# Late query tiles, context and mixing moved one head on; layer 1's output projection by token groups, its last norms woven with values

## The chip, the cores and the metric

The kernel runs on one core of a Trainium2 chip. The metric is the time of one execution in device microseconds; the median of three runs stands for the kernel. TensorE (PE in the profile) multiplies, VectorE (DVE), ScalarE (ACT) and GpSimd (POOL) work on elements, SyncE (SP) issues most DMAs.

## The reference

One inference step of a two-layer network over 1024 sample tokens and 128 prompt tokens, width 1024, all float32:

```python
for i in range(DEPTH):                       # DEPTH = 2
    sh1, sc1, g1, sh2, sc2, g2 = ada_modulation(cond, ada_w[i], ada_b[i])     # one set for prompt, one for sample
    h = modulate(x, norm_mix[i], sh1, sc1)
    if i % 2 == 0:     # pooling mixer of 4 channel groups beside latent attention of 8 heads, one output projection
        m = concatenate([pool_mixer(a_in, ...), attn]) @ w_out
    else:              # neighbourhood attention of 16 heads with learned bias, plus all prompt keys
        q, k, v = na_qkv(h, w_in_l1, na_q_norm, na_k_norm)                    # q and k normed for each head
        m = attn @ w_out_l1
    x = x + g1 * m
    x = x + g2 * channel_mixer(modulate(x, norm_mlp[i], sh2, sc2), mlp1[i], mlp2[i])   # squared relu, 4096 wide
```

`channel_mixer(h, w1, w2)` is `square(relu(h @ w1)) @ w2`. Queries and keys get an RMS norm over each head; prompt tokens attend to prompt tokens alone, sample tokens to sample and prompt.

## The kernel before

Activations lie with channels on the 128 partitions and the 1152 tokens along the free dimension, as eight tiles (KD = 8). Tokens are cut into three chunks of 384 (CH, NCH = 3) or four of 288 (HC); two chunks of 288 make a token group of 576. A float32 product is made from a high and a low part of each operand by three matmuls (`mm3`: low by high, high by low, high by high), so operands are split: ScalarE or VectorE casts the high part, VectorE or GpSimd subtracts it. `wsplit` does that for a weight chunk: a DMA of 512 KB to `wr`, a cast to `wh` (L160), a subtraction to `wl` (L161). Rings hold 3 `wr` and 4 each of `wh` and `wl`. Other buffers come from 36 slots of SBUF, `S.alloc` and `S.free`.

The program is written as generators; `weave` takes steps of several of them in proportion to the numbers beside them, and a scheduler orders each engine's queue from that by its own estimates. The order on each engine is thereafter fixed, and engines wait for each other by semaphores. PSUM tiles come from three pools, `pa`, `pb`, `pc`.

Layer 0. `query_tile(t)` norms one of six query tiles: for each chunk a pair of matmuls over 8 rows spreads the heads' factors over the partitions (`ps_b`, L707 and L708), VectorE multiplies (L808, L810), then the tile is split and stored (`split_store`, two DMAs). Tiles 0 to 3 hold the plain part of the heads' queries, two heads each, 4 and 5 the rotated part. All six run before the attention. Then `value_gen` (`ps_v`, L840 to L844) is woven with `max_units(0)`: for each 128 queries and each chunk one matmul (`ps_m`, L1073) and one reduction on VectorE (L1074), 24 units a head. `put_max` then transposes the maxima (`ps_mt`, L1059) and sends them over two DMAs on POOL's queue, `mrow<-row` and `qh<-mrow`, to row 96 of `qh`. `attend_units` makes scores from three matmuls (`ps_st`, L1108, L1111, and L1112, which reads that row), exponentials on ScalarE, and values (`ps_pv`, L1115). Each head h is woven with the maxima of head h + 2 (head 0 with those of 1 and 2), head 0 with `ctx0` (the prompt's attention) and head 1 with `mix` (pooling's matmuls). From head 1 on `background()` also runs `ada_gen`: VectorE makes the rest of layer 0's modulation from streamed weights (L200).

Layer 1. Queries and keys are made in four groups of four tiles; after each its norm block runs: sums of squares (`ps8`), `head_rstd` on VectorE (L252 to L704, to `r8h`, `r8l`), pairs of 8-row matmuls and products (L1266), three chunks by four tiles; then splits and stores. After group 3's, `value_gen1` (36 units of 24 matmuls of 256 columns, L1427 to L1429) is woven with `na_max` of heads 0 and 1. Of the 16 heads' output pairs, 0 to 6 go over HBM (`od`).

Output projection of layer 1. `split_acts` splits a pair in whole (`oh`, `ol`, L937 and L938). `out_first` takes pairs 0 to 3 over all tokens, 24 tiles of 12 matmuls of 384; 8 (OA) of them are woven with head 15. `out_second` takes pairs 4 to 7, 32 tiles of 12 matmuls of 288, chunk by chunk; from chunk 2 on it steps `operand_gen`, which makes the seven operands of the MLP's first products from the first group's tokens, each split at L352 and L353. Layer 0's projection has another form already: `split_groups` splits a pair by token group (`oa`, L914 and L915), and `out_group(0, g)` takes all eight pairs at once, 24 matmuls of 288 a tile; it runs group 0, then group 1 beside `operand_gen`. The MLP (`ps`, L446 to L482) starts with products of those operands.

Of the kernel before, what the change touches and what calls it, by code (L numbers as in the profile page):

```python
# [13 lines left out]
ALU = mybir.AluOpType  # L14
# [18 lines left out]
XS, PSH, OW, OA, OB = (11, 11, 12, 12, 13, 13, 14, 14), (14, 14, 15, 15), 10, 8, 6  # L33
# [57 lines left out]
def hybrid_kernel(ctx: ExitStack, tc: tile.TileContext, I, O):  # L91
# [783 lines left out]

    def out_first(layer, acts):
        for q in range(4):
            ws = wout_chunk(layer, 0, q)
            for mi in range(2):
                for ch in range(NCH):  # L880
                    ps = PS("ps_o")[:, :CH]
                    mm3(ps, ws[mi], acts, ch * CH, ch * CH + CH)
                    residual(x, 2 * q + mi, ch, ps, layer, 0)
                    yield

    def out_second(layer, acts):
        ws = [wout_chunk(layer, 1, q) for q in range(4)]
        st, right, ops, og = {}, [], {}, None
        for ch in range(4):
            for m in range(KD):  # L890
                if ch == 3 or ch == 2 and m in (3, 6):
                    next(og, None)
                ps = PS("ps_o", ("pa", "pc")[m % 2])[:, :HC]
                mm3(ps, ws[m // 2][m % 2], acts, ch * HC, ch * HC + HC)
                for a, b, i in chunk_parts(ch, HC):
                    nc.vector.scalar_tensor_tensor(x[m][:, a:b], ps[:, a - ch * HC:b - ch * HC], adav(layer, 2, m, i),
                                                   x[m][:, a:b], op0=ALU.mult, op1=ALU.add)
            if ch < 2:
                st[ch] = norm_stats(x, ch, HC)
            if ch == 1:  # L900
                og = operand_gen(ops, quad_apply(x, 0, layer, st[0]), right)
            elif ch == 2:
                right.extend(quad_apply(x, 1, layer, st[1]))
# [27 lines left out]

    def split_acts(ops):
        acts = []
        for o in ops:
            a = (S.alloc("oh", F32R), S.alloc("ol", F32R))
            acts.append(a)
            nc.vector.tensor_copy(a[0], o)  # L937
            nc.vector.tensor_sub(a[1], o, a[0])  # L938
            S.free(o)
        return acts  # L940

    def free_acts(acts):
        for a in acts:
            S.free(*a)
# [193 lines left out]
    for h in range(8):  # L1138
# [13 lines left out]
        if h in (0, 1):  # L1152
            gs.append(((ctx0, 8), (mix, 14))[h])
# [79 lines left out]
    r8 = S.alloc("r8h", F32R), S.alloc("r8l", F32R)  # L1233
    silu_load()
    for g in range(4):
# [16 lines left out]
        for ch in range(NCH):  # L1252
            cs = slice(ch * CH, ch * CH + CH)
            ps8 = PS("ps8", "pb")[0:8, :CH]
            for t in range(4):
                square_sum(ps8, t, raw[t][:, cs], t == 0, t == 3)
            head_rstd(ps8, 64, cs, nts[(NCH * g + ch) % 2], r8, rows)
        for ch in range(NCH):
            for t in range(4):
                wn = "naq" if t < 2 else "nak"  # L1260
                pp_ = pq if t < 2 else pk
                ps = PS("ps_b", "pb")[:, :CH]
                bcast(ps, t, r8, slice(ch * CH, ch * CH + CH), rows)
                for a, b, i in chunk_parts(ch):
                    o = pp_[:, pairs[t] * P:pairs[t] * P + P] if i else raw[t][:, a:b]
                    nc.vector.scalar_tensor_tensor(o, raw[t][:, a:b], V(wn), ps[:, a - ch * CH:b - ch * CH],  # L1266
                                                   op0=ALU.mult, op1=ALU.mult)
        for t in range(4):
            hi, lo = fhs[t % 2], raw[t].bitcast(F32R)
            nc.scalar.copy(hi[:, :NS], raw[t][:, :NS])  # L1270
            nc.vector.tensor_sub(lo[:, :NS], raw[t][:, :NS], hi[:, :NS])
            dst, o = (qd, 0) if t < 2 else (kd, P)
            dma(dst[0][pairs[t], :, o:o + NS], hi[:, :NS])
            dma(dst[1][pairs[t], :, o:o + NS], lo[:, :NS])
# [133 lines left out]


    vt = []  # L1410

    def value_gen1():
        for qt in range(4):
            ws = [wsplit(I["wv1"][qt, i]) for i in range(2)]
            fs = slice(qt * 256, qt * 256 + 256)
# [241 lines left out]
```

## Time and profile before

| | us |
|---|---|
| median of 3 runs | 2985.34 (2983.98 to 2985.49) |
| the profiled execution | 2996.6 |
| its span on the core | 2994.7 |
| TensorE busy | 2909.3 (97%) |
| VectorE busy | 2151.7 (72%) |
| ScalarE busy | 1321.2 (44%) |
| GpSimd busy | 329.3 (11%) |

The mean clock granted to TensorE was 0.977 of full speed. A busy share counts the time in which an instruction ran on the engine; matmuls overlap each other, so their own durations are longer than the distance between their starts, and pace is read from the starts or from counts in a window. Names in the rows are the program's, `out<-in`; `ps_b` is an output in PSUM, `bl`, `bh` the low and high part of an MLP operand.

### The profile page before, as it was taken

The page shows a single profiled execution, that of the slowest core. Times are in us where ns is not written, and L with a number is a line of the kernel's source. Part 1 is how long each engine was busy: PE and PEld are TensorE (multiplying, and loading weights), DVE is VectorE, ACT ScalarE, POOL GpSimd, SP SyncE. Part 2 cuts the span into 40 slices and gives each one's busy share as a digit, 9 for nine tenths or more (in the row PEclk, how much of TensorE's full clock was granted, in tenths as well). Part 3 has the DMA queues.
Part 4 walks back from the last instruction along what each step waited for, and adds up shares of the span by engine and source line. Part 5 has one row for each costly group of instructions (what it writes and reads, how often), then busy time and mean ns, then how long its engine had stood idle before and what let it go on. Part 6 is the DMA issues. An engine that isn't in the chain of part 4 may idle for free. (4 is left out here: it accounts for less than half of the span.)

```text
span 2994.7 us, 46426 instructions
## 1 busy us (share of the span) xinstructions
PE 2909.3 (97%) x18302; PEld 2610.2 (87%) x18302; DVE 2151.7 (72%) x3923; ACT 1321.2 (44%) x2136; POOL 329.3 (11%) x238
## 2 busy tenths in 40 slices
PE   7999999999999999999999999998989999999999
PEld 4955666799999999999988897666989999999999
DVE  5977863477778899786898524667587678877775
ACT  5463444345355544354644423444244445453433
POOL 2004010141000020000221000111020000200000
PEclk9997999999999999999999999898989999999999
DMA  6527521222232344233555325775213222332322
GB/s 236 170 86 254 144 76 41 77 77 88 84 105 77 101 141 148 78 99 92 170 204 183 116 101 128 194 187 165 70 36 99 80 91 85 117 101 78 98 78 89
DMA packets 117435, 347.59 MB, mean 116 GB/s; under 512 B 16697, under 2 KB 37801, under 8 KB 117218
## 3 DMA queue, kind: packets, MB, share of 16 engines
q1 hardware_dynamic: 114674, 340.76, 36.9%
q0 software_dynamic: 2544, 3.87, 0.4%
q8 instruction: 144, 2.36, 0.3%
q14 instruction: 73, 0.60, 0.1%
HBM read 296.54 MB, written 46.85 MB: 115 GB/s over the span
## 5 line engine op out<-in xcount | busy, mean ns | idle before, releaser
L477 PE MATMUL ps<-mh,wl 128*128 128x288 f32 x2048 | 599.8, 294 | 0.0
L478 PE MATMUL ps<-mh,wh 128*128 128x288 f32 x2048 | 595.6, 295 | 0.0
L476 PE MATMUL ps<-ml,wh 128*128 128x288 f32 x2048 | 590.4, 295 | 2.6 <-DVE x L482 1.4
L446 PE MATMUL ps<-bl,wh 128*128 128x288 f32 x1792 | 534.4, 299 | 16.1 <-DVE bl L353 5.2
L447 PE MATMUL ps<-bh,wl 128*128 128x288 f32 x1792 | 530.9, 296 | 0.0
L448 PE MATMUL ps<-bh,wh 128*128 128x288 f32 x1792 | 529.2, 295 | 0.0
L477 PEld LDWEIGHTS ps<-mh,wl 128*128 128x128 f32 x2048 | 384.2, 188 | 0.1
L476 PEld LDWEIGHTS ps<-ml,wh 128*128 128x128 f32 x2048 | 380.1, 188 | 3.6 <-DVE x L482 1.4
L478 PEld LDWEIGHTS ps<-mh,wh 128*128 128x128 f32 x2048 | 382.4, 188 | 0.0
L482 DVE SCALAR_TENSOR_TENSOR x<-ps,ada,x 128x288 f32<-128x288 f32 (+2 forms) x640 | 270.8, 451 | 122.7 <-PE ps L478 121.5
L446 PEld LDWEIGHTS ps<-bl,wh 128*128 128x128 f32 x1792 | 337.9, 189 | 20.5 <-issue 9.3
L448 PEld LDWEIGHTS ps<-bh,wh 128*128 128x128 f32 x1792 | 339.7, 190 | 0.0
L447 PEld LDWEIGHTS ps<-bh,wl 128*128 128x128 f32 x1792 | 338.8, 189 | 0.2
L160 ACT CAST wh<-wr 128x1024 fp32r<-128x1024 f32 x188 | 197.1, 1049 | 190.2 <-PE ps L448 77.3
L419 ACT CAST wh<-s 128x512 fp32r<-128x512 f32 x256 | 146.1, 618 | 278.6 <-PE ps L478 194.9
L161 DVE TENSOR_TENSOR wl<-wr,wh 128x1024 fp32r<-128x1024 f32 x144 | 179.2, 1248 | 60.1 <-ACT wh L160 60.1
L200 DVE CUSTOM_DVE_ANT_0 trash<-wada,silu 128x1024 bf16<-128x1024 f32 x160 | 206.1, 1288 | 13.3 <-DMA wada<-in_wada 6.9
L419 ACT CAST wh<-wr 128x1024 fp32r<-128x1024 f32 (+1 forms) x128 | 106.9, 835 | 199.7 <-PE ps L478 135.7
L161 POOL TENSOR_TENSOR wl<-wr,wh 128x1024 fp32r<-128x1024 f32 x44 | 117.2, 2670 | 689.8 <-ACT wh L160 689.8
L420 DVE TENSOR_TENSOR wl<-s,wh 128x512 fp32r<-128x512 f32 x232 | 157.2, 709 | 3.7 <-ACT wh L419 1.5
L1115 PE MATMUL ps_pv<-p,vt 128*128 128x512 f32 x288 | 147.7, 596 | 0.1
L1074 DVE TENSOR_REDUCE stat<-ps_m 128x1 f32<-128x384 f32 x192 | 98.6, 551 | 65.2 <-PE ps_m L1073 64.9
(321 smaller groups left out, 6044.2 us busy)
## 6 DMA issues: line engine op xcount, KB each, us to landing
wr<-in_w SPq DMA_DIRECT2D x256, 512.0 KB, 3.7
wada<-in_wada SPq DMA_DIRECT2D x48, 512.0 KB, 3.5
wada<-in_wada0t SPq DMA_DIRECT2D x32, 512.0 KB, 3.7
wr<-in_win SPq DMA_DIRECT2D x24, 512.0 KB, 4.5
wr<-in_wout SPq DMA_DIRECT2D x24, 512.0 KB, 4.3
kk<-kd SPq DMA_DIRECT2D x32, 288.0 KB, 7.3
wadan<-in_wada SPq DMA_DIRECT2D x16, 512.0 KB, 8.8
ta<-in_bias_q SPq DMA_DIRECT2D x16, 512.0 KB, 4.4
```

What stands on the lines that cost most here:

```text
L160: nc.scalar.copy(hi, r)
L161: (nc.gpsimd if e else nc.vector).tensor_sub(lo, r, hi)
L200: nc.vector.tensor_tensor_reduce(trash, r[:, :D], silu[i][:, :D], scale=1.0, scalar=0.0, op0=ALU.mult, op1=ALU.add, accum_out=a)
L419: nc.scalar.copy(h, src)
L420: (nc.gpsimd if j in EDGE and min(ps) in EDGE_POOL else nc.vector).tensor_sub(l, src, h)
L446: nc.tensor.matmul(ps, wh[:, a], hl[:, b], start=k == 0, stop=False)
L447: nc.tensor.matmul(ps, wl[:, a], hh[:, b], start=False, stop=False)
L448: nc.tensor.matmul(ps, wh[:, a], hh[:, b], start=False, stop=k == 3)
L476: nc.tensor.matmul(ps, wh, hl, start=kk == 0, stop=False)
L477: nc.tensor.matmul(ps, wl, hh, start=False, stop=False)
L478: nc.tensor.matmul(ps, wh, hh, start=False, stop=kk == 3)
L482: nc.vector.scalar_tensor_tensor(x[m][:, a:b], ps[:, a - ch * HC:b - ch * HC], g, x[m][:, a:b], op0=ALU.mult, op1=ALU.add)
```

## The change

Three places. In layer 0 only tile 1 still runs after 4 and 0; tiles 5, 2 and 3 become `late_queries`, woven with head 0. `ctx0` goes with head 1, `mix` with head 2, and the ada units start with head 2. In layer 1 the norm block becomes a generator, `norm_group`; that of group 3 is woven with the first nine units of `value_gen1`, and 27 units remain beside `na_max`. The output projection of layer 1 goes by token groups: `out_first` makes pairs 0 to 3 for group 0 alone (16 tiles of 12 matmuls of 288, 10 of them with head 15), `out_second` adds pairs 4 to 7 for group 0, then takes all eight pairs for group 1 (16 tiles of 24 matmuls) beside `operand_gen`, one step for two tiles. For that all eight weight chunks are loaded and split a second time.

```diff
-XS, PSH, OW, OA, OB = (11, 11, 12, 12, 13, 13, 14, 14), (14, 14, 15, 15), 10, 8, 6
+XS, PSH, OW, OA, OB = (11, 11, 12, 12, 13, 13, 14, 14), (14, 14, 15, 15), 10, 10, 6
...
-    for t in (1, 5, 2, 3):
-        run(query_tile(t, nc.gpsimd))
-    S.free(*rk8, bcs)
+    run(query_tile(1, nc.gpsimd))
+    def late_queries():
+        for t in (5, 2, 3):
+            yield from query_tile(t, nc.gpsimd)
+        S.free(*rk8, bcs)
+        yield
...
-        if h == 1:
+        if h == 2:
             silu_load()
             bg.append(chain(ada_gen(0, range(16 + 8 * NEARLY, 48)), free_silu()))
...
-        if h in (0, 1):
-            gs.append(((ctx0, 8), (mix, 14))[h])
+        if h < 3:
+            gs.append(((late_queries(), 13), (ctx0, 8), (mix, 14))[h])
...
+        norm = norm_group(g, raw, rows, pairs)
+        if g < 3:
+            run(norm)
+        else:
+            vg = value_gen1()
+            weave((norm, 10), (islice(vg, 9), 9))
...
-    weave((value_gen1(), 36), (chain(na_max(0, tls[0]), na_max(1, tls[1])), 10))
+    weave((vg, 27), (chain(na_max(0, tls[0]), na_max(1, tls[1])), 10))
...
     def out_first(layer, acts):
         for q in range(4):
             ws = wout_chunk(layer, 0, q)
             for mi in range(2):
-                for ch in range(NCH):
-                    ps = PS("ps_o")[:, :CH]
-                    mm3(ps, ws[mi], acts, ch * CH, ch * CH + CH)
-                    residual(x, 2 * q + mi, ch, ps, layer, 0)
+                for ch in range(2):
+                    out_tile(layer, 2 * q + mi, ch, ws[mi], acts, 0)
                     yield
...
     def out_second(layer, acts):
         ws = [wout_chunk(layer, 1, q) for q in range(4)]
-        for ch in range(4):
+        st = {}
+        for ch in range(2):
             for m in range(KD):
-                if ch == 3 or ch == 2 and m in (3, 6):
-                    next(og, None)
...
+                out_tile(layer, m, ch, ws[m // 2][m % 2], [a[0] for a in acts[4:]], 1)
+            st[ch] = norm_stats(x, ch, HC)
+        for a in acts[4:]:
+            S.free_ap(a[0][0])
+        ops = {}
+        og = operand_gen(ops, quad_apply(x, 0, layer, st[0]), quad_apply(x, 1, layer, st[1]))
+        n = 0
+        for q in range(4):
+            ws = [wout_chunk(layer, half, q) for half in range(2)]
+            for mi in range(2):
+                for ch in (2, 3):
+                    out_tile(layer, 2 * q + mi, ch, [w for half in range(2) for w in ws[half][mi]], [a[1] for a in acts], 1)
+                    n += 1
+                    if n % 2 == 0:
+                        next(og, None)
...
-            acts = split_acts(pairs)
-            of = out_first(1, acts)
+            acts = [split_groups(o) for o in pairs]
+            of = out_first(1, [a[0] for a in acts])
```

`out_tile` makes one tile of 288 tokens by `mm3` and adds it to `x` on VectorE. Line numbers in the changed program differ: L1073 becomes L1069, L1059 L1055, L1108 to L1115 L1104 to L1111, L1427 to L1429 L1283 to L1285, L896 L880.

The first place is TensorE's queue between the transposing matmul of head 0's maxima and the first score matmul that reads them (L1112). Before:

```order
L1073 MATMUL ps_m<-kh_2107,qh_2106 128x384
L1059 MATMUL ps_mt<-ident,stat 8x128
L1073 MATMUL ps_m<-kh_2114,qh_2113 128x384 x2
L1108 MATMUL ps_st<-qh_2106,kl_2193 128x512
L1111 MATMUL ps_st<-ql_2192,kh_2107 128x512
L1073 MATMUL ps_m<-kh_2114,qh_2113 128x384 x3
L1108 MATMUL ps_st<-qh_2106,kl_2193 128x512
L1111 MATMUL ps_st<-ql_2192,kh_2107 128x512
L1073 MATMUL ps_m<-kh_2114,qh_2113 128x384 x13
L1112 MATMUL ps_st<-qh_2106,kh_2107 128x512 x3
L1073 MATMUL ps_m<-kh_2114,qh_2113 128x384 x3
L1115 MATMUL ps_pv<-p_2364,vt_241_2093 128x512
```

In the changed kernel, where that matmul is L1108:

```order
L1055 MATMUL ps_mt<-ident,stat 8x128
L1069 MATMUL ps_m<-kh_2114,qh_2113 128x384 x2
L1104 MATMUL ps_st<-qh_2106,kl_2139 128x512
L1107 MATMUL ps_st<-ql_2138,kh_2107 128x512
L1069 MATMUL ps_m<-kh_2114,qh_2113 128x384 x2
L707 MATMUL ps_b<-rkh_1463,bcs_1407 128x384
L708 MATMUL ps_b<-rkl_1464,bcs_1407 128x384
L1069 MATMUL ps_m<-kh_2114,qh_2113 128x384
L1104 MATMUL ps_st<-qh_2106,kl_2139 128x512
L1107 MATMUL ps_st<-ql_2138,kh_2107 128x512
L1069 MATMUL ps_m<-kh_2114,qh_2113 128x384 x3
L1108 MATMUL ps_st<-qh_2106,kh_2107 128x512 x3
```

Eight maxima and a broadcast pair stand between them in place of 18 maxima, and the other late pairs are spread through head 0.

The second is TensorE's queue in the norm block of group 3 (L707, L708) and the first values (`ps_v`). Before, from the last sum of squares on:

```order
L327 MATMUL ps_16527<-sql,sel8r 8x384
...
L1429 MATMUL ps_v_16828<-wh,hh_948_13874 128x256
L707 MATMUL ps_b<-r8h_14389,bcs_14365 128x384
L708 MATMUL ps_b<-r8l_14390,bcs_14365 128x384
...
L707 MATMUL ps_b<-r8h_14389,bcs_14365 128x384 x3
L708 MATMUL ps_b<-r8l_14390,bcs_14365 128x384 x3
L707 MATMUL ps_b<-r8h_14389,bcs_14365 128x384
L708 MATMUL ps_b<-r8l_14390,bcs_14365 128x384
L1320 MATMUL ps_m<-kk_16653,qq_16654 128x256
...
L1427 MATMUL ps_v_16854<-wl,hh_941_13867 128x256
```

And after, from the second unit of values, where the third chunk's pairs begin:

```order
L1285 MATMUL ps_v_16830<-wh,hh_948_13874 128x256
L1283 MATMUL ps_v_16864<-wl,hh_941_13867 128x256
L1284 MATMUL ps_v_16864<-wh,hl_949_13875 128x256
L707 MATMUL ps_b<-r8h_14389,bcs_14365 128x384 x2
L1285 MATMUL ps_v_16864<-wh,hh_941_13867 128x256
...
L1285 MATMUL ps_v_16864<-wh,hh_942_13868 128x256
L708 MATMUL ps_b<-r8l_14390,bcs_14365 128x384 x2
L1283 MATMUL ps_v_16864<-wl,hh_943_13869 128x256
...
L707 MATMUL ps_b<-r8h_14389,bcs_14365 128x384
L708 MATMUL ps_b<-r8l_14390,bcs_14365 128x384
L1283 MATMUL ps_v_16864<-wl,hh_944_13870 128x256
```

Values now stand ahead of and between the pairs, which stood together before, ahead of nearly all values.

The third is VectorE's queue at the end of layer 1's output projection: the splits of the MLP operands (L353), the additions to `x` (L896, later L880), and the first work of the MLP (L452). Before:

```order
L896 SCALAR_TENSOR_TENSOR x_1404_19748<-ps_o,ada_92,x_1404_19748 128x160
L353 TENSOR_TENSOR bl_20807<-t_1494_20788,bh_20806 128x1152
L381 TENSOR_TENSOR hq_20769<-hq_20770,hq_20769 128x1152
L896 SCALAR_TENSOR_TENSOR x_1404_19748<-ps_o,ada_92,x_1404_19748 128x128
L410 TENSOR_TENSOR s_21217<-wr 128x512
L353 TENSOR_TENSOR bl_20827<-hq_20769,bh_20826 128x1152
L353 TENSOR_TENSOR bl_20846<-t_1493_20787,bh_20845 128x1152
L388 TENSOR_TENSOR hq_20632<-hq_20632,t_1494_20788 128x1152
L452 TENSOR_TENSOR u_20965<-ps_20981,scr_20966 128x288
L453 TENSOR_TENSOR scr_20966<-ps_20995,scr_20966 128x288
L353 TENSOR_TENSOR bl_20866<-hq_20632,bh_20865 128x1152
L353 TENSOR_TENSOR bl_20885<-hq_20770,bh_20884 128x1152
```

After:

```order
L353 TENSOR_TENSOR bl_20812<-t_1494_20755,bh_20811 128x1152
...
L353 TENSOR_TENSOR bl_20882<-hq_20545,bh_20881 128x1152
L353 TENSOR_TENSOR bl_20939<-t_1493_20754,bh_20938 128x1152
L388 TENSOR_TENSOR hq_20528<-hq_20528,t_1494_20755 128x1152
...
L353 TENSOR_TENSOR bl_21009<-hq_20528,bh_21008 128x1152
L353 TENSOR_TENSOR bl_21066<-hq_20546,bh_21065 128x1152
L880 SCALAR_TENSOR_TENSOR x_1403_19746<-ps_o,ada_92,x_1403_19746 128x288
...
L880 SCALAR_TENSOR_TENSOR x_1403_19746<-ps_o,ada_92,x_1403_19746 128x128
L880 SCALAR_TENSOR_TENSOR x_1404_19748<-ps_o,ada_92,x_1404_19748 128x288
...
L880 SCALAR_TENSOR_TENSOR x_1404_19748<-ps_o,ada_92,x_1404_19748 128x128
...
L452 TENSOR_TENSOR u_21101<-ps_21117,scr_21102 128x288
```

The splits, the last four of which stood behind the last addition and two of them behind the MLP's own first work, now all stand ahead of the last addition.

More of the change, by code (lines that the diff above doesn't have):

```diff
@@ L874, in wout_chunk, with out_tile @@
                  for k in range(4)] for m in range(2)]
+    def out_tile(layer, m, ch, ws, acts, k):
+        ps = PS("ps_o", ("pa", "pc")[m % 2] if k else "pa")[:, :HC]
+        mm3(ps, ws, acts, ch % 2 * HC, ch % 2 * HC + HC)
+        for a, b, i in chunk_parts(ch, HC):
+            nc.vector.scalar_tensor_tensor(x[m][:, a:b], ps[:, a - ch * HC:b - ch * HC], adav(layer, 2, m, i),
+                                           x[m][:, a:b], op0=ALU.mult, op1=ALU.add)
     def out_first(layer, acts):
@@ L887, in out_second @@
         ws = [wout_chunk(layer, 1, q) for q in range(4)]
-        st, right, ops, og = {}, [], {}, None
-        for ch in range(4):
+        st = {}
+        for ch in range(2):
             for m in range(KD):
-                if ch == 3 or ch == 2 and m in (3, 6):
-                    next(og, None)
[L893 to L903, printed above, removed]
+                out_tile(layer, m, ch, ws[m // 2][m % 2], [a[0] for a in acts[4:]], 1)
[13 more added lines that the diff above has]
+                        next(og, None)
         run(og)
-        free_acts(acts)
+        for a in acts:
+            S.free_ap(a[1][0])
         return ops
@@ L930, in out_group @@
                                                        adav(layer, 2, m, i), x[m][:, a:b], op0=ALU.mult, op1=ALU.add)
[L932 to L944, printed above, removed]
     def prompt_softmax(ps, nh, scale, w, o):
@@ L1251, in hybrid_kernel @@
             background(QBG)
[L1252 to L1274, printed above, removed]
+        norm = norm_group(g, raw, rows, pairs)
+        if g < 3:
+            run(norm)
+        else:
+            vg = value_gen1()
+            weave((norm, 10), (islice(vg, 9), 9))
         if g == 2:
@@ L1512, in hybrid_kernel @@
     run(of)
-    free_acts(acts)
-    acts = split_acts(pairs + opairs[7:])
+    for a in acts:
+        S.free_ap(a[0][0])
+    acts += [split_groups(o) for o in pairs + opairs[7:]]
     ops = out_second(1, acts)
```

74 lines of the change are left out of this document (50 added, 24 removed).

## The prediction, made before the changed kernel had run

> **What bounds the kernel.** I read the page first: the share of each engine, the 40 slices, the clock row.
>
> ```profile
> span 2994.7 us, 46426 instructions
> PE 2909.3 (97%) x18302; PEld 2610.2 (87%) x18302; DVE 2151.7 (72%) x3923; ACT 1321.2 (44%) x2136; POOL 329.3 (11%) x238
> ...
> PE   7999999999999999999999999998989999999999
> ...
> PEclk9997999999999999999999999898989999999999
> ```
>
> TensorE is busy 97% of the span, so the time is the number of matmuls times their pace, plus the few places where TensorE stands or runs at a lower clock. The profiled execution took 2996.6 us (span 2994.7), 11.3 us over the 2985.3 us median; I sum against the profile and subtract from the median, since 0.4% changes no term by 0.1 us. Next I asked what TensorE waited for; columns are total, times, longest.
>
> ```profile
> PE ps L446 <- DVE bl L353: 5.2, 1, 5.2
> ...
> PE ps_b L707 <- DVE r8h L703: 2.5, 1, 2.5
> ```
>
> The first is the start of layer 1's MLP, the second its last norm group: parts C and B of the change. Then busy time by stretch, for each part.
>
> **A, the late query tiles.**
>
> ```profile
> core 0: us, PE busy (x) PEld busy (x) DVE busy (x) ACT busy (x) POOL busy (x), PEclk, DMA share, GB/s
> 252.20:257.00 4.80, 4.71 (x14) 4.21 (x14) 4.48 (x10) 2.72 (x5) 2.22 (x1) 0.50 1.02 419
> 276.60:286.00 9.40, 8.96 (x24) 6.22 (x25) 7.80 (x17) 0.26 (x1) 1.24 (x2) 0.68 0.80 190
> 286.00:328.30 42.30, 40.53 (x161) 26.57 (x160) 23.55 (x49) 18.83 (x43) 1.03 (x2) 0.94 0.32 90
> 328.30:372.40 44.10, 42.12 (x156) 29.50 (x156) 43.01 (x78) 22.46 (x37) 3.40 (x3) 0.96 0.56 158
> 372.40:405.30 32.90, 32.10 (x113) 20.55 (x113) 27.19 (x49) 13.73 (x23) 3.48 (x3) 1.00 0.40 117
> 405.30:437.60 32.30, 32.30 (x116) 21.22 (x115) 14.56 (x28) 12.17 (x21) 1.03 (x2) 1.00 0.20 53
> ```
>
> From the timeline (start, us, engine, line, operation):
>
> ```profile
> 257.04 0.80 PE L840 MATMUL ps_v<-wl,ckh 128*128 128x512 f32 x1
> 263.67 1.09 PE L1073 MATMUL ps_m<-kh,qh 96*128 96x384 f32 x3
> ...
> 258.34 1.10 SPq L113 DMA_DIRECT2D qh<-qdn  x2
> ```
>
> Nine broadcast pairs go; the values would start some 6 us earlier than 257.04. But the maxima behind them need qh, whose load SP issues at 258.34 only, behind tile 1's store, which stays; the DMA share there is 1.02. Three tiles' stores no longer compete, so the load lands sooner: between nothing and 4.9 us (263.67 less 258.8, the second issue's rough time). I take -2, nearer to nothing, because DMA is full at 419 GB/s.
>
> Now the heads, which end at the borders of those windows. Head 3 carries nothing extra: 32.3 us. Head 0 has ctx0 and some of head 1's and 2's maxima (42.3), head 1 has mixing and 21 ada units (44.1, VectorE 43.0 busy: VectorE bounds it), head 2 has ten ada units.
>
> ```profile
> L200 DVE CUSTOM_DVE_ANT_0 trash<-wada,silu 128x1024 bf16<-128x1024 f32 x21 | 27.2, 1294 | 0.5 <-DMA wada<-in_wada0t 0.4
> ```
>
> That group is VectorE's ada work in head 1. Four places of the timeline:
>
> ```profile
> 264.44 3.81 DVE L1074 TENSOR_REDUCE stat<-ps_m 128x1 f32<-128x384 f32 x8 [6.56 <-PE ps_m L1073]
> ...
> 276.61 0.38 PE L1059 MATMUL ps_mt<-ident,stat 128*8 128x128 f32 x1 [0.86 <-DVE stat L1055]
> ...
> 277.48 0.63 PE L1108 MATMUL ps_st<-qh,kl 96*128 96x512 f32 x1
> 277.91 0.63 PE L1111 MATMUL ps_st<-ql,kh 96*128 96x512 f32 x1
> ...
> 285.99 1.48 PE L1112 MATMUL ps_st<-qh,kh 97*128 97x512 f32 x3
> ...
> 2136.92 0.34 PE L337 MATMUL ps_o<-oh,wh 128*128 128x384 f32 x1
> ...
> 2137.96 0.33 PE L337 MATMUL ps_o<-oh,wh 128*128 128x384 f32 x1
> ```
>
> The last two rows give the pace of a 384-column matmul: six lie between their starts, 1.04 us, 0.173 each. The maxima's row gives VectorE's pace where nothing else is in its queue, 3.81 / 8 = 0.48 each.
>
> ctx0's price is taken as 5 us of head 0's 10 above head 3 (the rest is maxima); an error in it cancels, since it leaves head 0 and enters head 1, which loses mixing and its ada units: 32.4 + 5 = 37.5. Head 2 gets mixing and 17 ada units: VectorE 14.6 + 22.0 (17 by 1.294) + 1.2 (43.0 - 14.6 - 27.2 is what mixing adds) = 38, with head 1's slack some 43.5 in place of 44.1. Head 3 gets eight ada units (10.4) on its 14.6 of VectorE: covered, 33. So heads 1 to 3 take 114 against 109.3: +4.7. The tail loses 0.5. Head 0: -5 for ctx0; 18 matmuls of the pairs at 0.173, +3.1; and a wait. From the transposing matmul (276.61) to the first scores that need the row of maxima (285.99) pass 9.4 us, a chain through two DMAs. 18 maxima of head 1 filled it; now eight, a pair and four score matmuls: 8 x 0.48 = 3.8 us on VectorE, 5.9 if the four score matmuls (0.43 each between the starts at 277.48 and 277.91) and the pair don't run beside it, so 3.5 to 5.6 us short. VectorE then catches the ten others up beside head 0, where it is busy 23.6 of 42.3; on TensorE they cost 10 x 0.173 = +1.7. The late tiles' own VectorE work (about 5 us) and stores hide in the same slack; without it they cost that. POOL now issues head 0's row first and a tile's 2.4 us of subtraction behind it, so no late tile delays the row. On SP the late tiles' six stores go behind head 1's loads; their first reader is head 4's load of queries, two heads on. Sum: -2 - 5 + 3.1 + 1.7 + 4.7 - 0.5 = **+2**. Ends: pairs and wait wholly absorbed, -3; late tiles' VectorE work uncovered as well, +7.
>
> What a wait does to the clock is seen in part B's rows: 2.5 us of it, then 0.50.
>
> ```profile
> 1722.32 1.33 PE L707 MATMUL ps_b<-r8h,bcs 8*128 8x384 f32 x3 [2.51 <-DVE r8h L703]
> ```
>
> ```profile
> 1718.30:1725.80 7.50, 4.69 (x17) 3.14 (x15) 5.98 (x14) 2.85 (x5) 0.61 (x2) 0.68 0.00 1
> 1725.80:1731.30 5.50, 5.50 (x25) 5.28 (x25) 5.38 (x10) 3.58 (x6) 0.94 (x3) 0.50 0.90 356
> 1740.00:1745.50 5.50, 5.50 (x46) 5.23 (x45) 2.59 (x5) 0.66 (x2) 0.42 (x1) 1.00 0.71 212
> ```
>
> [...] Head 0 already ran at 0.94, so I add nothing.
>
> **B, norms woven with values.** Only group 3's norms change. Before: eight pairs of 8-row matmuls, in their midst a 2.5 us wait for the third chunk's VectorE chain, then half clock till 1731.3. 5.50 us held 25 matmuls there and 46 at full clock. Now 52 value matmuls (0.12 each) and four pairs stand ahead of the third chunk's first pair: 52 x 0.12 + 8 x 0.17 = 7.6 us, more than that chain, which ran from the chunk's last sums at about 1717.4 to 1722.32. Gain: the wait, 2.5, and half of the 9.0 us from 1722.32 to 1731.30, 4.5; 7.0 in all. I take **-6.5** (the pairs' VectorE products of 0.6 us each still come at their own pace, which the values need not cover to the end). Ends: -8 and, if the chain is late again, -3.
>
> **C, output projection by token groups.**
>
> ```profile
> 2124.30:2137.70 13.40, 13.40 (x81) 13.37 (x80) 9.94 (x14) 3.76 (x4) 2.39 (x1) 1.00 0.12 39
> 2205.00:2240.00 35.00, 25.55 (x144) 24.41 (x143) 28.41 (x33) 14.24 (x20) 13.19 (x8) 0.76 0.16 46
> 662.00:697.00 35.00, 33.80 (x248) 32.92 (x247) 28.61 (x40) 19.96 (x29) 13.82 (x8) 1.00 0.26 81
> 705.00:740.00 35.00, 35.00 (x266) 35.00 (x265) 23.62 (x41) 10.80 (x17) 0.00 (x0) 1.00 0.21 60
> ...
> 2150.00:2205.00 55.00, 55.00 (x404) 54.79 (x403) 40.29 (x79) 24.23 (x47) 11.65 (x9) 1.00 0.06 20
> ```
>
> And the chain of the last pair, on POOL and VectorE:
>
> ```profile
> 2128.31 2.39 POOL L1084 TENSOR_TENSOR den<-den,ry 128x1024 f32<-128x1024 f32 x1 [37.47 <-ACT ry L1083]
> ...
> 2136.38 1.35 DVE L938 TENSOR_TENSOR ol<-no,oh 128x1152 fp32r<-128x1152 f32 x1
> ```
>
> The first 35 us of layer 1's MLP hold 144 matmuls; at full pace 266 fit, 0.132 us each: 122 x 0.132 = 16.0 us lost, because its operands are split on VectorE late. Layer 0's MLP, whose out_group(0, 1) already gives it ready operands, lost (266 - 248) x 0.132 = 2.3. In the new order all seven operand splits (L353) stand on VectorE before the last residual, so layer 1 loses about as much: **-13.7**. Against it: 768 matmuls of 288 columns at 0.133 (102.1) replace 288 of 384 at 0.173 and 384 of 288 (100.9): +1.2. Eight more weight chunks cost ACT 1.05 and VectorE 1.25 each, 10 us beside 51 us of group 1's matmuls (384 by 0.133); their loads, 512 KB each on SP, meet a DMA share of 0.06.
>
> ```profile
> L160 ACT CAST wh<-wr 128x1024 fp32r<-128x1024 f32 x188 | 197.1, 1049 | 190.2 <-PE ps L448 77.3
> ...
> L161 DVE TENSOR_TENSOR wl<-wr,wh 128x1024 fp32r<-128x1024 f32 x144 | 179.2, 1248 | 60.1 <-ACT wh L160 60.1
> ...
> L938 DVE TENSOR_TENSOR ol<-op,oh 128x1152 fp32r<-128x1152 f32 x7 | 9.3, 1351 | 0.1
> L915 DVE TENSOR_TENSOR oa<-o,oa 128x576 fp32r<-128x576 f32 x8 | 7.9, 1024 | 0.1
> ```
>
> VectorE's instructions there, from the first operand split to the last residual, add up to about 43 us by the mean durations of their groups; the cover is 51, and today VectorE is 40 of 55 busy, so they hide; if they don't, each costs its 1.25. Splitting a pair in halves takes 2 x 1.02 for 1.35; in head 15, where TensorE waits for a split already, +1. The last pair needs 13.4 us from its last values (2124.30) to its split (2137.70); 95 matmuls (12.6 us) cover it now: +1, up to +3. Sum **-10.5**; ends -15 and -5.
>
> **Sum.** +2 - 6.5 - 10.5 = -15: 2985.3 - 15 = **2970**.
>
> **Rivals.** (1) A gains too: pairs and wait fit gaps of heads 0 to 2, A -5 in place of +2: 2963. For it: head 0's VectorE is 56% busy. Against: TensorE is 96% busy there. (2) C's gain is given back: VectorE is late in group 1's part through the extra chunks and the MLP starts as before, C +3, with A and B as summed: 2 - 6.5 + 3 = -1.5, 2984. For it: VectorE is 40.3 of 55 us busy there already, and 10 us come on top. Against: 51 us for 43, and layer 0 runs so. (3) B's chain isn't covered, since value units wait for PSUM or weights: B 0 and a total of 2977; against it stands the order's 7.6 us. (4) Slower: operand buffers come free only with group 1's last tile, so the operand splits run behind it. Half of the 28.4 us that VectorE was busy at 2205 to 2240 would be added to the old 16: C +16 (those 14 and the +1 to +3 for columns and splits) and 2985.3 + 2 - 6.5 + 16 = 2997. It decides once over 20 us of VectorE's operand work lie behind the last output matmul. Against it: the splits stand ahead of it in the order, and layer 0 holds as many buffers.
>
> **Chances.** Forecast (2964 to 2978) 0.55, (1) 0.13, (2) 0.14, (3) 0.10, (4) 0.08. A change under 0.2%, 6 us, can't be told from none. Faster: 0.53 + 0.13 + 0.09 + 0.03 = 0.78; same: 0.02 + 0.01 + 0.10 = 0.13; slower 0.09 with what is left of (2). The range 2957 to 2986 leaves out the lower half of (1) and all of (4). The forecast's own range, 2964 to 2978, is A's, B's and C's ends taken half way together.
>
> **What would show it.** A: head 0's maxima start at 261 to 263; TensorE stands 2 to 4 us before the first three-fold scores; head 1 takes 37 to 38 us, head 2 43 to 44. B: no r8h wait over 1 us in group 3, clock 1.00 through the values. C: the first 35 us of layer 1's MLP hold 240 matmuls or more, and no wait for bl above 1 us. The prediction fails if that count stays below 200, or heads 0 to 3 grow by over 8 us together.

## The result, and the profile after

The changed kernel takes 2971.55 us (median of 5 runs, 2966.75 to 2974.66); the kernel before, on the same chip, 2985.49 (5 runs, 2983.98 to 2993.57). The ratio is 0.9938, with a 95% interval of 0.9922 to 0.9954: faster by some 0.6%, and the median 1.6 us from the forecast 2970. The medians differ by 13.9 us; the ratio, an estimate from all the runs, stands for 18.5; two of the five runs before took 2993 us. The profiled execution is the one that took 2971.55. Its page:

```profile
span 2969.4 us, 46660 instructions
...
PE 2891.8 (97%) x18398; PEld 2592.8 (87%) x18398; DVE 2160.1 (73%) x3931; ACT 1327.8 (45%) x2144; POOL 328.4 (11%) x238
...
PEclk9997999999999999999999999999999999999999
```

TensorE has 96 matmuls more (18398 for 18302) and is busy 17.5 us less (2891.8 for 2909.3). Matmuls overlap (at B's place one of 256 columns lasts 0.28 us and the next starts 0.12 us after it), so I read the change from starts of single matmuls, the same ones in both traces:

| stretch | before, us | after, us | |
|---|---|---|---|
| start to head 0's first maximum | 263.67 | 260.08 | -3.6 |
| to the last value matmul of layer 0's heads | 296.58 | 302.00 | +5.4 |
| to layer 1's first value matmul (`ps_v`) | 1133.75 | 1134.02 | +0.3 |
| to the last of them | 127.19 | 122.72 | -4.5 |
| layer 1's heads, to their last value matmul (`ps_pv`) | 303.06 | 292.69 | -10.4 |
| to the MLP's first matmul on a `bl` | 78.50 | 84.87 | +6.4 |
| to the 100th such matmul after it | 84.79 | 65.97 | -18.8 |
| to the end | 707.11 | 707.08 | 0.0 |

So in these traces A gives +1.8 (first two rows), B -4.5, C -12.4 (the two before the last), and layer 1's heads, which the change does not touch, -10.4. The spans differ by 25.3, the medians by 13.9: the profiled execution of before was 11 us over its median, and the heads' row is most of that, as the experiments show.

Busy time by stretch, after; the borders of the heads lie at the same events as in the forecast's windows. The first row is the maxima, the second from the transposing matmul to the first three-fold scores, then heads 0 to 3, two rows of B and two of C:

```profile
core 0: us, PE busy (x) PEld busy (x) DVE busy (x) ACT busy (x) POOL busy (x), PEclk, DMA share, GB/s
260.00:273.00 13.00, 11.68 (x28) 6.25 (x26) 11.52 (x25) 1.90 (x4) 2.36 (x1) 0.71 0.84 220
273.00:278.80 5.80, 5.77 (x16) 4.53 (x17) 3.60 (x7) 0.25 (x1) 1.24 (x2) 0.50 0.01 1
278.80:323.30 44.50, 44.49 (x149) 27.39 (x147) 27.79 (x57) 14.44 (x24) 8.22 (x5) 0.92 0.33 106
323.30:367.00 43.70, 40.14 (x166) 26.24 (x167) 28.55 (x56) 20.69 (x48) 2.10 (x4) 1.00 0.53 154
367.00:407.30 40.30, 38.79 (x145) 26.26 (x143) 39.11 (x65) 22.86 (x36) 4.75 (x2) 1.00 0.49 144
407.30:439.50 32.20, 31.61 (x112) 20.63 (x113) 26.95 (x57) 12.16 (x21) 1.09 (x2) 1.00 0.40 121
1718.00:1726.00 8.00, 8.00 (x51) 6.30 (x49) 4.91 (x9) 2.32 (x5) 0.00 (x0) 1.00 0.27 67
1726.00:1732.00 6.00, 6.00 (x36) 4.60 (x37) 2.11 (x7) 1.26 (x2) 0.42 (x1) 1.00 0.01 3
...
2145.00:2196.40 51.40, 51.40 (x389) 51.29 (x388) 44.75 (x70) 24.74 (x38) 9.78 (x5) 1.00 0.24 73
2196.00:2231.00 35.00, 34.94 (x261) 34.50 (x260) 27.01 (x39) 20.43 (x30) 14.28 (x9) 1.00 0.30 91
```

The second row answers to 276.60:286.00 before, 9.4 us: now 5.8, and TensorE works through it. The 1718 and 1726 rows are B's place, where before TensorE stood 2.5 us and then ran at clock 0.50: now no gap and clock 1.00. The last two are C: VectorE 44.75 of 51.4 us busy under group 1's output tiles, and 261 matmuls in the MLP's first 35 us, where there were 144, a dozen of them still the projection's.

### The profile page after: what moved, and what is told of

Same layout as the page of the kernel before. It is cut to its first block, busy times and chain, and to the rows that moved or that the text cites. A ratio compares the mean times of both kernels' runs of the same rounds, so it can differ in the third digit from the quotient of the medians.

```text
span 2969.4 us, 46660 instructions
## 1 busy us (share of the span) xinstructions
PE 2891.8 (97%) x18398; PEld 2592.8 (87%) x18398; DVE 2160.1 (73%) x3931; ACT 1327.8 (45%) x2144; POOL 328.4 (11%) x238
## 5 line engine op out<-in xcount | busy, mean ns | idle before, releaser
L160 ACT CAST wh<-wr 128x1024 fp32r<-128x1024 f32 x196 | 205.2, 1049 | 173.6 <-PE ps L448 77.6
L161 DVE TENSOR_TENSOR wl<-wr,wh 128x1024 fp32r<-128x1024 f32 x152 | 188.9, 1246 | 46.6 <-ACT wh L160 46.5
L335 PE MATMUL ps_o<-oa,wh 128*128 128x288 f32 x512 | 153.1, 300 | 3.2 <-DVE oa L925 2.5
L336 PE MATMUL ps_o<-oa,wl 128*128 128x288 f32 x512 | 152.6, 298 | 0.0
```

What stands on the lines that cost most here:

```text
L160: nc.scalar.copy(hi, r)
L161: (nc.gpsimd if e else nc.vector).tensor_sub(lo, r, hi)
L335: nc.tensor.matmul(ps, wh, hl[:, c0:c1], start=k == 0, stop=False)
```

## The experiments

Runs of one kernel spread by 7 to 22 us (the kernel before, 34 runs on one chip: 2980.17 to 2997.80), so where a kernel ran once I read only the stretches of its trace that repeat. Over the traces of kernels with the same code there, B's stretch repeats within 0.3 us, and so do C's two, with two exceptions: the values in B alone (124.2 us for 122.7) and the MLP's start in A alone (80.4 us for 84.8). Layer 0 up to the end of its heads repeats less well, within 2.8 us with A and 0.7 without.

**The three parts apart.** Each part alone, and B with C: e1 is the kernel before with the first place changed, e2 with the second, e3 with the third, and e4 is the changed kernel with the first place as before.

```diff
 # e1_A
+            gs.append(((late_queries(), 13), (ctx0, 8), (mix, 14))[h])
...
 # e2_B
+            vg = value_gen1()
+            weave((norm, 10), (islice(vg, 9), 9))
...
 # e3_C
+                    out_tile(layer, 2 * q + mi, ch, [w for half in range(2) for w in ws[half][mi]], [a[1] for a in acts], 1)
...
 # e4_BC, against the changed kernel
-    run(query_tile(1, nc.gpsimd))
+    for t in (1, 5, 2, 3):
+        run(query_tile(t, nc.gpsimd))
...
```

> Only part A: the three late query tiles with head 0, ctx0 with head 1, mixing and the ada units from head 2. Theory (heads 0 to 7 of the two traces): head 7 ends 1.85 us later, because nine woven pairs cost 0.74 us each where they cost 0.64 in a row at half clock; so 2987.3, +2 us, between 0 and +4. Rival: the heads of layer 1, which gained 10 us in the trace of after and are not touched, gained because something before them moved; then A alone may show part of it, -3 us or more. A third, that A pays as it was drawn (4.7 us of pairs gone): -5.

Measured: 2986.96 us (12 runs) against 2986.29 (34 runs), ratio 1.0005 (0.9992 to 1.0019). From the start to the end of layer 0's heads 564.6 us, against 560.2 before: 4.4 us later, where the changed kernel's trace has 1.8.

> Only part B: group 3's norms woven with nine units of values. Theory: -4.5 us, the distance from the first to the last value matmul in the two traces (126.95 and 122.48 us); TensorE never stands between 1710 and 1745, at clock 1.00. Rival: layer 1's heads start in another phase of their loads and the 10 us that they gained in the trace belong to B; then -10 to -15. As predicted: -6.5.

Measured: 2986.40 (12 runs), ratio 0.9998 (0.9985 to 1.0011). Its values took 124.2 us for 127.2.

> Only part C: layer 1's output projection by token groups. Theory: the MLP's start loses nothing (16.0 us before), and some 2.5 us go to columns and to splits in head 15: -13, between -10 and -16; the first 35 us of layer 1's MLP hold 255 to 262 matmuls. Rival: head 15 and the heads before it carry the gain; then the MLP's start gives the same count but the time moves by less than 8 or more than 18 us.

Measured: 2973.39 (11 runs), ratio 0.9958 (0.9945 to 0.9971), -12.5 us. By its trace C's two stretches take 150.84 us for 163.29, -12.45.

> The changed kernel without part A. Theory: parts add, -4.5 - 13 = -17.5 against before, 2 us faster than with A (2969.6). Rival: A's trace hides a gain (layer 1's heads): then 3 us or more slower than with A.

Measured: 2975.03 (12 runs), ratio 0.9955 (0.9939 to 0.9972), -13.4 us.

A can't be told from zero, and C carries the gain; time (-16.4 to -8.7 us) and trace agree on its size. B's 3 to 4.5 us are seen in every trace that has it unaltered, and its interval in time (-4.5 to +3.3 us) has them only at its edge. By the ratios the parts add up to -11.6 us, A +1.5, B -0.6, C -12.5, while the whole measured -18.5 (-23.3 to -13.7). By the medians they add up to -12.1, and the whole is -13.9, so most of the 7 us lies in how the runs are summed up. B with C was expected 2 us faster than the changed kernel; its median is 3.5 us slower, which would speak for the rival that A hides a gain, but the two intervals overlap, and this stays open. No trace shows work of one part that another part shortens; I put the rest down to chance in the heads below, without proof.

The heads of layer 1 have the same code in all these kernels, but for C's output tiles beside head 15. Busy time of that stretch (columns as above), in the trace of before:

```profile
1821.20:2124.20 303.00, 276.54 (x1142) 190.63 (x1141) 203.90 (x506) 120.20 (x222) 36.51 (x44) 0.91 0.68 178
```

of B alone:

```profile
1814.70:2119.80 305.10, 278.43 (x1142) 190.75 (x1141) 205.22 (x506) 120.22 (x222) 36.42 (x44) 0.91 0.68 176
```

of A alone:

```profile
1824.67:2113.42 288.75, 265.75 (x1142) 183.99 (x1141) 204.13 (x506) 120.10 (x222) 36.51 (x44) 0.95 0.69 186
```

and of B with C:

```profile
1812.40:2101.90 289.50, 263.19 (x1169) 181.17 (x1167) 206.27 (x520) 121.31 (x223) 36.42 (x44) 0.96 0.71 188
```

The first three have the same 1142 matmuls and 506 VectorE instructions, and 303, 305 and 289 us, with granted clocks of 0.91, 0.91 and 0.95. TensorE stands 23 to 27 us of each, in short waits, the longest of them for DMAs. So the stretch differs by 16 us between traces with the same order, and with it the clock. These are three kernels with one trace each; but executions of one kernel differ in the same way: of the 34 runs of before, the six fastest had clocks of 0.980 to 0.982, the six slowest 0.976 to 0.979. Why the clock differs from run to run, and which wait goes with the lower clock, no trace here shows.

**The place of the operand splits.** If C gains because the seven operand splits stand ahead of the last additions on VectorE, then holding them back must give the gain back. e5 holds the last four of the seven, and two of the differences between operands, behind the last addition; e11 holds all seven and all the differences (`r` is the last addition to `x`; the order is VectorE's queue order, with no new semaphore). Nothing else is changed.

```diff
         def step(i):
+            if hold:
+                after(i, hold[0])
...
-                    if n % 2 == 0:
+                    if n % 2 == 0 and n <= 8:     # e11 has neither this line nor the next
                         next(og, None)
+        hold.append(r)
         run(og)
```

> The changed kernel with the last four of the seven operand splits ordered behind the last addition of the output projection, where they stood before; all else in the same order. Theory: C's gain is the place of these splits: the stretch from the MLP's first product to its hundredth low-part matmul grows from 65.97 back towards 84.8 us, by 12 to 18 us. Rival: the gain comes from the weights' buffers or from the groups' order itself; then the stretch stays within 3 us of 65.97.

> As the kernel with four late splits, but all seven operand splits and the differences between operands stand behind the last addition. Theory: the 11.5 us of C's gain that four late splits did not give back come from the operand work ahead of them on VectorE; the stretch from the MLP's first product to its hundredth low-part matmul then grows from 73.2 to 80 us or more, or the first product starts 8 us or more later after the last head's values (84.9). Rival: they come from the weights and the groups' order; then both stay within 3 us of 73.2 and 84.9.

Measured once each, 2985.06 and 2992.60 us. Busy time in the MLP's first 35 us of e5:

```profile
2202.70:2237.70 35.00, 30.01 (x206) 28.73 (x206) 30.53 (x37) 18.32 (x26) 12.58 (x8) 0.95 0.22 70
```

TensorE's wait for the operands in e5 (total, times, longest):

```profile
PE ps L448 <- DVE bl L353: 3.2, 2, 1.9
```

The same stretch of e11:

```profile
2205.30:2240.30 35.00, 27.73 (x168) 26.99 (x169) 29.39 (x32) 16.35 (x22) 8.26 (x5) 0.80 0.19 60
```

and its wait:

```profile
PE ps L448 <- DVE bl L353: 8.4, 2, 4.9
```

261, 206 and 168 matmuls with no, four and seven splits late. To the 100th matmul on a `bl` the MLP takes 65.97, 73.23 and 78.10 us; with e11's later first matmul (+3.6) the loss is 15.8, which turns C's -12.4 into +3.3. So the place of the operand work on VectorE is worth more than C's whole gain. Both runs missed what was expected of them: e5's loss, 7.3, is less than 12 to 18, and e11, at 78.1 us with a first matmul 3.6 us later, stayed below its 80 us and 8 us, though above the rival's 3. e5 is also not the state of before. There the third split, VectorE's row in before, ended only at 2214.4, long after the MLP's first matmul at 2202.75:

```profile
2211.20 3.19 DVE L353 TENSOR_TENSOR bl<-t,bh 128x1152 fp32r<-128x1152 f32 x1
```

So two operands were ready before and three in e5. That the MLP has work while the rest come is what I take for the reason of e5's smaller loss; no run holds back five.

**The price of a woven pair.** In the changed kernel, at B's place (PE's timeline: start, duration, line):

```profile
1716.35 0.28 PE L1285 MATMUL ps_v<-wh,hh 128*128 128x256 f32 x1
1716.56 0.44 PE L707 MATMUL ps_b<-r8h,bcs 8*128 8x384 f32 x1
1716.84 0.33 PE L708 MATMUL ps_b<-r8l,bcs 8*128 8x384 f32 x1
1717.11 0.38 PE L1283 MATMUL ps_v<-wl,hh 128*128 128x256 f32 x1
1717.33 0.28 PE L1284 MATMUL ps_v<-wh,hl 128*128 128x256 f32 x1
```

From start to start: 0.21 for the value matmul ahead (0.12 is its pace), 0.55 for the pair, 0.22 for the value matmul behind. With what the neighbours lose, that is 0.09 + 0.55 + 0.10 = 0.74 us of TensorE for a pair, where the forecast had 0.35. e6 gives group 3's pairs all 128 rows, 120 of them zeros, so that no two neighbours differ in rows (`r8z` is zeroed once, and its rows 0 to 7 written):

```diff
+    nc.gpsimd.memset(bcs.bitcast(F32), 0.0)
...
+            r8z = S.alloc("r8zh", F32R), S.alloc("r8zl", F32R)
+            norm = norm_group(g, raw, rows, pairs, r8z, slice(0, P))
```

> The changed kernel with the broadcast pairs of group 3 over 128 rows (the other 120 are zeros) in place of 8. Theory: B gained 4.5 instead of 7 us since a woven pair costs 0.74 us (0.09 before it, 0.545, 0.10 behind it) where it costs 0.35 among pairs, and this is a price of changing between 8 and 128 rows; then a pair's two starts take 0.35 and its neighbours 0.12, and the stretch from the first to the last value matmul falls from 122.7 to about 118. Rival: the price comes with any change of weights' or outputs' form; then no change, 122 to 123.

PE's timeline of e6 at the same place:

```profile
1712.02 0.28 PE L1287 MATMUL ps_v<-wh,hh 128*128 128x256 f32 x1
1712.14 0.34 PE L707 MATMUL ps_b<-r8zh,bcs 128*128 128x384 f32 x1
1712.32 0.33 PE L708 MATMUL ps_b<-r8zl,bcs 128*128 128x384 f32 x1
1712.49 0.28 PE L1285 MATMUL ps_v<-wl,hh 128*128 128x256 f32 x1
1712.61 0.28 PE L1286 MATMUL ps_v<-wh,hl 128*128 128x256 f32 x1
```

A pair of 128 rows takes 0.35, and both neighbours 0.12: the 0.39 us on top of a pair's own time is the price of going from 128 rows to 8 and back. What TensorE does in these 0.39 us, no trace here shows. The whole kernel took 2974.81 in one run, and its values 126.2 us, where about 118 were expected and the changed kernel has 122.7: TensorE now waits in that stretch, 2.3 us for ScalarE's evacuation of the values and 3.2 us for VectorE's reductions of the maxima that share it, none of which the changed kernel's trace has. So taking the price away gained nothing here.

**Where ada stands in A.** e7 is the changed kernel with the ada units from head 1 on, as before.

```diff
-        if h == 2:
+        if h == 1:
             silu_load()
```

> The changed kernel with the ada units starting with head 1 again. Theory: A's loss of 2 to 4 us comes from its woven pairs (9 by 0.74, against 0.64 in a row) and not from VectorE's ada units; the stretch from head 0's first maximum to head 7's last value stays between 300 and 304 us (302.0). Rival, as predicted: heads 1 to 3 lose 4.7 us by the ada units being pressed into head 2; then the stretch falls below 299.

Layer 0's heads took 317.3 us, 15 more than in the changed kernel and more than was expected either way; one run, 2981.68. Busy time in head 1 of e7:

```profile
328.50:385.40 56.90, 42.96 (x162) 27.71 (x162) 46.72 (x92) 20.15 (x46) 2.10 (x4) 0.88 0.58 170
```

VectorE's group of ada units there:

```profile
L200 DVE CUSTOM_DVE_ANT_0 trash<-wada,silu 128x1024 bf16<-128x1024 f32 x25 | 30.4, 1217 | 3.8 <-DMA wada<-in_wada0t 3.5
```

and TensorE's longest wait there:

```profile
PE ps_m L1069 <- DMA ctxqk<-ctxqk: 7.7, 1, 7.7
```

56.9 us for 43.7. VectorE has 30.4 us of ada; TensorE waits 7.7 us ahead of a maximum, and about 4 for the context's softmax on VectorE. The row of the longest wait names the load of the context's queries and keys, but that matmul reads `kh` and `qh`, whose loads SP issued between 330.11 and 333.94, in among the context's (321.09 to 334.63); it started at 337.27. In this order the context and the ada units can't share a head without loss: A without that move cost 15 us more, in one run.

**A better version.** In layer 1's heads of the changed kernel TensorE waits most for the row of maxima (`q<-mrow`, 12.9 us, longest 8.0), which goes to HBM and back by two DMAs. e8 sends the row by one DMA from SBUF to SBUF, in both layers. e9 gives layer 0's query pairs 128 rows. e10 has both and leaves A out; e12 is e10 with the two DMAs.

```diff
 # e8, and in e10
-        r = cst.tile([P, P], F32R, tag="row", name="row")
+        r = cst.tile([P, P], F32R, tag="row", name="row", bufs=2)
-        dma(d, r[0:8, 0:P], nc.gpsimd)
...
-            dma(dst, d.rearrange("a b -> (a b)").unsqueeze(0), nc.gpsimd)
+            dma(dst, r[0:8, 0:P], nc.gpsimd)
...
 # e9, and in e10 and e12
-            bcast(ps, t, rk8, slice(ch * CH, ch * CH + CH), qrows)
+            bcast(ps, t, rk8, slice(ch * CH, ch * CH + CH), slice(0, P))
...
```

> The changed kernel with the maxima's row taken by one DMA from SBUF to SBUF in place of two over HBM (layers 0 and 1). Theory: the 17 us between fast and slow executions, and the 10 us that layer 1's heads gained in the trace of after, are the landing of these rows (1.6 to 8.9 us after issue); without the first of the two DMAs the stretch from the last value unit to the last head's values falls below 288 us (289 to 305 in six traces), its spread over runs halves, and the median falls by 5 to 15 us. Rival: other loads (qq, bias, exponentials) set these heads and the rows only come last; then the stretch stays at 290 to 300 and the median within 4 us of the changed kernel's.

Measured: 2964.53 (6 runs, 2955.50 to 2971.85), ratio 0.9929 (0.9907 to 0.9950). Layer 0's heads fell by 3.0 us, but layer 1's, at 293.7, stayed in the rival's 290 to 300 and did not fall below 288, and the runs spread as before (16 us). Beside the changed kernel (0.9922 to 0.9954) it can't be told apart.

> The changed kernel with layer 0's query pairs over 128 rows (zeros in the others) in place of 8. Theory: matmuls of 8 rows hold the clock at half from 243 to 259 us although TensorE is busy, and cost 0.74 us a pair when woven; with 128 rows the pairs that stand in a row take 0.35 us each instead of 0.64, those woven 0.35 instead of 0.74, and the stretch from head 0's first maximum to head 7's last value falls from 302 to 298 us, to where it was without A (296.2) plus the pairs. Rival: the clock stays at half for another reason (VectorE or the waits around it) and the pairs' rows don't matter; then 302 stays.

One run, 2976.36. Layer 0's heads took 298.0 us for 302.0, as expected; but head 0's maxima began 2.9 us later, where TensorE waited 5.4 us for ScalarE's evacuation of the values, in place of 4.0.

> Parts B and C without A, the row of maxima by one DMA, and layer 0's pairs over 128 rows. Theory: B and C -17 by segments, some 5 of them (B) lost again in layer 1's heads, pairs -3: 2968, between 2960 and 2975, the first maxima at 260 to 262 us. Rival, that A pays once its pairs are cheap: then this stays 3 us or more behind the changed kernel's 0.9938.

Measured: 2956.77 (6 runs, 2950.70 to 2966.29), ratio 0.9900 (0.9876 to 0.9923): the best here, and faster than the 2960 to 2975 expected; its first maxima came at 264.8 us, not 260 to 262. It beats the changed kernel: its slowest run, 2966.29, is below that one's fastest, 2966.75, though on another chip.

> Parts B and C without A and layer 0's pairs over 128 rows, but the row of maxima over HBM by two DMAs as before: the last kernel that was timed at 0.990 without its direct row. Theory: the direct row is worth what that one won over B and C alone (0.9955), since layer 1's heads then wait and halve the clock less; so the ratio goes back to 0.994 to 0.997 and the stretch of layer 1's heads to 288 to 300 us. Rival: the direct row is idle and the 18 us are layer 0's pairs or the spread of the heads: then the ratio stays at 0.989 to 0.992.

Measured: 2974.01 (5 runs), ratio 0.9958 (0.9944 to 0.9972). TensorE's wait for the row in layer 1's heads of e12:

```profile
PE ps_st L1389 <- DMA q<-mrow: 11.5, 3, 8.2
```

and of e10:

```profile
PE ps_st L1388 <- DMA q<-row: 0.3, 1, 0.3
```

11.5 us of waits become 0.3, though TensorE's other waits there grow by about 4.5, and the kernel is 17 us faster (0.9958 to 0.9900). The direct row is shown to be what makes e10 fast. How its 17 us come about is not: in the two profiled executions, whose spans differ by 14.2 us, layer 0's heads end 5.6 us earlier (1.9 of it lies ahead of the first row), layer 1's take 5.6 less (282.8 for 288.3, at a granted clock of 0.95 for 0.94), and 3.0 fall to the layers' stages between, which the row does not touch. Why the same edit can't be told from none beside A, in e8, is open too.

## Why the prediction was right, and where its steps were not

The change came out as forecast because C, which carries it, worked as it was drawn. That the total is off by 1.6 us only is in part luck: B gave 2.0 us less than summed and C 2.0 more, and A's errors cancel within it.

**A, forecast +2, measured +1.8 in the two traces and +1.5 (-2.4 to +5.7) by time.** In the five traces that have A as drawn (the changed kernel, e1, e5, e6, e11) layer 0's heads end 1.7 to 4.5 us later than before, so that forecast and trace agree to 0.2 us is chance. The sum held through errors that cancel, and one of my own marks failed: heads 0 to 3 together take 160.7 us for 151.6, +9.1, where I wrote that over 8 would refute me. Against them stand -3.6 at the start and -3.7 in the chain to the scores.

The start: the values begin earlier by 4.4 us (252.61 for 257.04), not 6, since with the pairs gone TensorE has nothing to fill a wait for ScalarE. PE's timeline, after:

```profile
252.61 0.80 PE L840 MATMUL ps_v<-wl,ckh 128*128 128x512 f32 x1 [4.02 <-ACT vt L850]
260.08 1.08 PE L1069 MATMUL ps_m<-kh,qh 96*128 96x384 f32 x3
273.03 0.38 PE L1055 MATMUL ps_mt<-ident,stat 128*8 128x128 f32 x1 [0.86 <-DVE stat L1051]
278.76 1.48 PE L1108 MATMUL ps_st<-qh,kh 97*128 97x512 f32 x3
```

The maxima start at 260.08, 3.6 earlier (I took 2, of 0 to 4.9).

The wait: I took the 9.4 us from 276.61 to 285.99 as the chain's own length, and counted a wait of 3.5 to 5.6 in the place of work taken out. There is no wait: 273.03 to 278.76 is 5.7 us, filled. Nor did the chain end the 9.4 us before: the row landed 2.5 us after the load's issue at 283.15, 0.4 us ahead of the scores, and TensorE's own queue, its last maxima 0.47 us apart, filled the time. But the chain was nearly as long, and it became shorter: from the transposing matmul to the landing it took 9.0 us, and now 5.0 (issue at 276.06, 2.0 us to land). With the old chain TensorE would have waited some 3.3 us. POOL's two issues in the timeline, before:

```profile
277.58 0.71 POOL L113 DMA_DIRECT2D mrow<-row  x1 [10.14 <-DMA kh<-kdn]
283.15 0.53 POOL L113 DMA_DIRECT2D qh<-mrow  x1 [4.86 <-DMA mrow<-row]
```

and after:

```profile
274.00 0.71 POOL L113 DMA_DIRECT2D mrow<-row  x1 [10.20 <-ACT row L1057]
276.06 0.53 POOL L113 DMA_DIRECT2D qh<-mrow  x1 [1.35 <-DMA mrow<-row]
```

From the one to the other 5.57 us became 2.06. The DMA share in that stretch was 0.80 before and is 0.01 now: SP issued twelve loads of the context's queries and keys from 275.15 to 286, which now come with `ctx0` in head 1, from 323.32 on, and the late tiles' first store comes at 290.67. The five traces without A that send the row over HBM have 4.9 to 5.7 us from issue to issue, the seven with A 2.1; no run changes the traffic alone. A duration that contains a DMA was carried over to a place with other traffic: that was the failed step. For the clock behind that wait I added nothing; there was no wait ahead of head 0's scores, so no run here shows what one does to the clock at that place. The clock was 0.50 in the 5.8 us, with TensorE busy, and 0.92 in head 0.

The heads: the pairs cost 0.74 us each at full clock, not 0.35, and head 0 takes 44.5 us, +2.2. Head 1 takes 43.7, not 37 to 38. Four of TensorE's groups there:

```profile
L982 PE MATMUL ps_s<-ctxqk,ctxqk 96*128 96x128 f32 x16 | 2.5, 278 | 0.7 <-DMA ctxqk<-ctxqk 0.7
L988 PE MATMUL ps_po<-ctxw,vp 128*64 128x128 f32 x16 | 1.3, 285 | 0.0
L958 PE MATMUL ps_t<-ident,ctxw 128*128 128x128 f32 x8 | 1.3, 286 | 1.0 <-DVE ctxw L954 1.0
L335 PE MATMUL ps_p<-pl,wh 128*128 128x384 f32 x2 | 0.8, 390 | 1.6 <-DVE pl L862 1.6
```

`ctx0` is busy 5.1 us (2.5 + 1.3 + 1.3), the 5 that I took; but the sum for head 1 left out its waits (0.7 + 1.0) and mixing's first matmuls, which the weave puts here, with 1.6 of wait. These make some 4 of the 6 us; the rest no row here names. Head 2 took 40.3 for 43.5, with VectorE busy 39.1 of them, the bound I named; head 3 the 32 it had. My four heads came to 42.1 + 37.4 + 43.5 + 33 = 156, +4.4 (the forecast rounded head 1 up to 37.5); they took +9.1.

**B, forecast -6.5, measured -4.5 in the trace.** The mechanism was right: no gap, clock 1.00, rival 3 excluded by the two rows above. What is missing is a term: the sum took a pair's matmuls at 0.17 each before and after, and gave weaving no price. A woven pair costs 0.74, as e6 shows, 0.39 above 0.35; for the eight that stood together before and are woven now that is 3.1 us, more than the 2.0 by which I missed, and the eight together paid some of it already (the value matmul ahead of them, at 1717.66 in before, took 0.21 us for 0.12).

**C, forecast -10.5, measured -12.45 in the trace and -12.5 in time.** Both terms have to be read with one correction: before, the MLP's first matmul on a `bl` stood ahead of the last of the output projection. TensorE's groups in before from 2202.70 to 2240:

```profile
L336 PE MATMUL ps_o<-oh,wl 128*128 128x288 f32 x9 | 2.7, 295 | 0.0
L337 PE MATMUL ps_o<-oh,wh 128*128 128x288 f32 x9 | 2.7, 295 | 0.0
L335 PE MATMUL ps_o<-ol,wh 128*128 128x288 f32 x8 | 2.4, 295 | 0.0
```

24 of these 26 start behind the MLP's first, 24 x 0.133 = 3.2 us, and after none does. So the projection costs +6.4 - 3.2 = +3.2, as summed (1.2 + 1 + 1), though by other items: 1.2 for the columns, 1.3 because 142 matmuls of 288 columns start ahead of the heads' end where 117 of 384 did (117 x 0.173 less 142 x 0.133), and a gap of 0.8 at 2124.2, where the last pair's split ends. The MLP's start gives -18.8 + 3.2 = -15.6 for -13.7: I had taken layer 0's 248 of 266 as the end, and it reaches 261. VectorE is busy 44.75 of 51.4 us, against the 43 of 51 that I added up: the cover held, with 6.6 us to spare. This refutes rivals 2 and 4. e11 built the state of rival 4 by hand, every split behind the last addition, and there C becomes +3.3, not the +16 that I priced: half of VectorE's 28.4 us was added to the old loss of 16, in which five splits that came too late were counted already.

**What I had no term for** is the spread of layer 1's heads, 288 to 305 us over the twelve traces in which their code is the same (those output tiles apart): the two profiled executions differ by 10.4 us there, more than by A and B together. I compared with the median instead of the profile, which kept it out of the forecast; anyone who subtracts the two profiles would credit the change with 25 us.

## What to carry to other kernels

Where a stage starts with operands made on another engine, move the making ahead of the last results of the stage before, and add up the cover: here 45 us of VectorE under 51 of TensorE, worth 16 us at the MLP's start, while dearer matmuls cost 3. A chain with a DMA in it has no length of its own here (5.57 us from issue to issue at a DMA share of 0.80, 2.06 at 0.01); take its price with the traffic it will meet. A small row that goes over HBM and back can be worth a direct DMA: 17 us without A, nothing that can be told from the spread with it. Before a gain is read from two traces, look at a stretch that the change does not touch.

## What was not expected of the hardware

- A pair of 8-row matmuls between 128-row ones cost 0.74 us of TensorE in the changed kernel, and with 128 rows (zeros in the rest) 0.35 in e6.
- Whether 8-row matmuls hold the clock down is open. Before, TensorE was busy 4.71 of 4.80 us with them at 252.2, at 0.50, and the clock from 240 to 256 us was 0.60. In e10, with 128 rows, it was 0.89 there, although TensorE was idle for a third of the time:

```profile
240.00:256.00 16.00, 10.29 (x35) 6.96 (x36) 15.04 (x32) 6.93 (x11) 6.09 (x6) 0.89 0.90 332
```

But in e9 TensorE was busy 4.74 of 4.80 us with pairs of 128 rows (243.5 to 248.3), and the clock was 0.50 as well; so the rows alone do not decide it.
- The row of maxima took 2.06 us from its store's issue to its load's at a DMA share of 0.01, and 5.57 at 0.80; without the way over HBM, e10 is 17 us faster than e12.
